# A linear-attention trunk on one core: the fourth chunk matrix made behind the solve, inverse steps over sixteen gaps, output transposes a chunk later, the last residuals in one load

## The chip, the core and the metric

One NeuronCore of a Trainium2 chip runs the whole program: TensorE (PE, with its weight loads as PEld), VectorE (DVE), ScalarE (ACT), GpSimd (POOL), and SyncE (SP), which issues most DMAs. The metric is the device time of one execution in microseconds (us). Each engine runs its instructions in the order in which they stand in its queue, and waits on semaphores.

## The reference, cut to what matters

A sequence of 2048 tokens with 1024 features is normed, modulated and projected. Half of the projection goes through a recurrent mixer (RWKV-7: 8 heads with a 64 x 64 state each), half through banded attention; both are gated, projected by `w_out`, and added to x.

```
def rwkv7_step(state, inp):
    r_t, w_t, k_t, v_t, a_t, b_t = inp
    sa = jnp.einsum('bhij,bhj->bhi', state, a_t)
    state = state * w_t[:, :, None, :] + sa[..., None] * b_t[:, :, None, :] + v_t[..., None] * k_t[:, :, None, :]
    y = jnp.einsum('bhij,bhj->bhi', state, r_t)
    return state, y
...
y = jnp.concatenate([y_r * jax.nn.silu(g_r), y_a * jax.nn.silu(g_a)], axis=-1)
x = x + gate[:, None, :] * (y @ w_out[l])
```

## The kernel before

The recurrence is computed in 32 chunks of 64 tokens (`NCH`), four to a block of 256 tokens (`NCB` = 4, `TR` = 256, `NB` = 8). Within a chunk the step over time becomes a triangular system; only the 64 x 64 state z goes from chunk to chunk. The change lies in `phase_r`, the loop over the chunks, which runs from about 1278 us to the end. What comes before it (projections, attention, and the first two blocks' matrices) is not touched.

Per block b there are these tiles and tensors: `ar` and `kb` (1 MB each, loaded from DRAM by `prefetch`), `g` (the chunk matrices, four chunks of eight heads), `l_d` and `xt_d` (small DRAM tensors through which 32 x 32 diagonal blocks change their layout). The chain that makes a block ready is:

- `qchunk(b, c)` (L191): 16 matmuls into `ps_q` and two masks on DVE (L206) make chunk c's matrix in `g`. After the fourth chunk, SP stores the diagonal blocks to `l_d` (L210, four DMAs).
- `inv(b)` (L218): SP loads a unit matrix into `xtt` (L221) and the diagonals into `lt` (L223); DVE inverts them in 31 steps of two instructions, `pd` (L229) and `xtt` (L231); SP stores the result to `xt_d` (L234) and reads it back into `g` (L237, four DMAs).
- `turn(b)` (L855): DVE transposes the inverted blocks into x. `merge1(n)` and `merge2(n)` (PE, with ACT copies between) then complete chunk n's inverse.

A chunk n runs on PE in this order: `from_state` (L891, L894, with the state z), `state_keys` for the next chunk, `solve` (L904), `merge1` of the next chunk, `state` (L912, after which DVE makes the new z, L914 and L915), `read_out` (L923), `values` for the next two chunks at odd n, `merge2`, `qchunk` of block b+2, `from_values` (L884). At the last chunk of a block (a border), `turn` and `merge1` of the next block stand late, after `read_out`.

Between these stand gaps. `gap()` does two things: it takes one step of `fill`, a generator that does the output projection (`outputs`; three matmuls of 512 columns into `ps_out`, L130 to L132, eight groups of four steps to a job), and it calls `invert()`, which takes as many steps of the inverse as its count of calls allows. There are six calls of `invert` in a chunk, so 24 in a block. The output of a pair of chunks goes through `square` (ACT) and `spread` (DVE, then POOL) after the second chunk; in the next, even chunk follow `scaled` (L942, DVE on ys), `flip` (L947, PE transposes and four ACT pieces L950 into yf), and `gated` (L955, L956, DVE, and a store to `yr_d`). The residual of each output group is loaded into one of three `xres` buffers (L1012), added on DVE (L1027), and stored by POOL's queue (L1028).

In this phase PE, DVE and ACT keep the order in which the code is written; SP and POOL are ordered by a scheduler. The two lines that pace the inverse are

```
work.update(inv=q_["inv"](b + 1) if b + 1 < NB else iter(()), calls=0, done=0)   # at the first chunk of block b
want = min(32, max(0, 5 * (work["calls"] - 4) // 2))
```

that is, inverse b+1 starts in block b at the fifth call, two and a half steps a call, and its 32nd item (the stores) falls to the 17th.

## Time and profile before

| | us |
|---|---|
| median of three runs (1746.02, 1747.77, 1752.72) | 1747.77 |
| the profiled execution | 1754.3 |
| its span, first to last instruction | 1752.5 |
| PE busy | 1564.3 (89%) |
| DVE busy | 1087.3 (62%) |
| ACT busy | 929.8 (53%) |
| mean granted TensorE clock | 0.947 |

The recurrent phase is the last quarter of the span. An engine's busy share over the whole span says little of it, since the stages before have other limits. Therefore the rows below are taken from stretches of that phase: by chunk, by block, and by the DMAs that lead from one block to the next. A granted clock of 1 is 2.4 GHz, of 0.5 it is 1.2 GHz; a mean between them says that the stretch had parts at both. In the tables of stretches, x is the number of instructions.

### The profile page before, as it was taken

The numbers are of one execution on the slowest core, as the hardware profiler recorded it, in microseconds if no ns is written. First come the engines' busy times: TensorE is split into PE (matmuls) and PEld (weight loads), VectorE is DVE, ScalarE is ACT, GpSimd is POOL, SyncE is SP. The second block draws the span as 40 slices with busy tenths as digits, with TensorE's granted clock in tenths as the row PEclk, the third lists the DMA queues.
The fourth block names the chain that finished last, engine by engine and source line by source line (L and its number), as shares of the span: only waits on it lengthen the run. The fifth ranks groups of instructions, "written<-read, shape, count | busy, mean of one in ns | idle before, by whom it ended". The sixth has DMA issues, their size and how long they took to land.

```text
span 1752.5 us, 32125 instructions
## 1 busy us (share of the span) xinstructions
PE 1564.3 (89%) x11944; PEld 1280.5 (73%) x11944; DVE 1087.3 (62%) x2435; ACT 929.8 (53%) x2087; POOL 674.2 (38%) x543
## 2 busy tenths in 40 slices
PE   3899999899999799999979999987889889988895
PEld 2677877688778678878868888866667767776775
DVE  7546457475576857557485574575965677656642
ACT  3666556566565566656656565662244344443550
POOL 4456545465454455544435543332401111111112
PEclk9899999799999999999999999998988998889998
DMA  8463332332324423132242323146576665654533
GB/s 288 122 222 101 115 111 89 128 103 86 114 85 141 158 86 127 67 109 97 79 127 78 122 76 99 55 144 197 173 221 187 176 196 159 187 163 131 151 120 99
DMA packets 188956, 231.59 MB, mean 132 GB/s; under 512 B 62976, under 2 KB 101632, under 8 KB 188800
## 3 DMA queue, kind: packets, MB, share of 16 engines
q1 hardware_dynamic: 183552, 212.76, 39.9%
q0 software_dynamic: 5248, 16.78, 2.6%
q8 instruction: 94, 1.54, 0.4%
q14 instruction: 62, 0.51, 0.1%
HBM read 171.30 MB, written 58.20 MB: 131 GB/s over the span
## 4 chain that ended last, share of the span: by engine, by line
PE 57%; DVE 21%; DMA 8%; issue 6%; ACT 4%; POOL 1%; SPq 1%; POOLq 0%; DVEq 0%; ACTq 0%
PE ps_qkvg L130 6%; PE ps_qkvg L131 6%; PE ps_qkvg L132 6%; PE ps_r L130 5%; PE ps_r L131 5%; PE ps_r L132 5%; PE ps_pt L604 2%; DVE pd L229 2%; DVE xtt L231 2%; PE ps_o L613 2%; DVE kbt L318 2%; PE ps_o L612 2%; DMA g<-xt_d 2%; PE ps_sa L567 2%; PE ps_out L130 1%
## 5 line engine op out<-in xcount | busy, mean ns | idle before, releaser
L111 POOL TENSOR_TENSOR wlo<-raw,whi 128x512 fp32r<-128x512 f32 x272 | 369.6, 1363 | 438.9 <-ACT whi L122 384.4
L122 ACT CAST whi<-raw 128x512 fp32r<-128x512 f32 x272 | 167.7, 618 | 176.8 <-issue 58.0
L130 PE MATMUL ps_r<-hh,whi 128*128 128x512 f32 x544 | 219.1, 403 | 11.1 <-ACT carry L641 9.7
L132 PE MATMUL ps_r<-hh,wlo 128*128 128x512 f32 x544 | 217.9, 401 | 2.3 <-POOL wlo L111 2.2
L131 PE MATMUL ps_r<-hl,whi 128*128 128x512 f32 x544 | 217.7, 400 | 0.0
L130 PE MATMUL ps_qkvg<-hh,whi 128*128 128x512 f32 x480 | 197.4, 413 | 11.6 <-ACT carry L641 7.3
L131 PE MATMUL ps_qkvg<-hl,whi 128*128 128x512 f32 x480 | 194.5, 406 | 7.9 <-DVE hl L386 5.5
L132 PE MATMUL ps_qkvg<-hh,wlo 128*128 128x512 f32 x480 | 193.2, 404 | 0.4 <-POOL wlo L111 0.3
L111 DVE TENSOR_TENSOR ptl<-ps_pt,pth 128x384 fp32r<-128x384 f32 (+1 forms) x232 | 105.3, 472 | 43.8 <-ACT pth L607 43.3
L597 ACT ACTIVATE sp<-sp,mn 128x640 f32<-128x640 f32 (+4 forms) x128 | 97.9, 765 | 63.8 <-DVE mn L593 62.9
L130 PEld LDWEIGHTS ps_r<-hh,whi 128*128 128x128 f32 x544 | 103.3, 190 | 31.6 <-ACT carry L641 10.6
L132 PEld LDWEIGHTS ps_r<-hh,wlo 128*128 128x128 f32 x544 | 102.9, 189 | 24.8 <-POOL wlo L111 3.1
L131 PEld LDWEIGHTS ps_r<-hl,whi 128*128 128x128 f32 x544 | 103.2, 190 | 20.1
L130 PEld LDWEIGHTS ps_qkvg<-hh,whi 128*128 128x128 f32 x480 | 92.5, 193 | 33.6 <-ACT carry L641 8.8
L131 PEld LDWEIGHTS ps_qkvg<-hl,whi 128*128 128x128 f32 x480 | 92.6, 193 | 30.3 <-DVE hl L386 7.6
L607 ACT CAST pth<-ps_pt 128x384 fp32r<-128x384 f32 (+1 forms) x232 | 90.8, 415 | 43.5 <-PE ps_pt L604 38.8
L132 PEld LDWEIGHTS ps_qkvg<-hh,wlo 128*128 128x128 f32 x480 | 92.3, 192 | 21.1 <-POOL wlo L111 0.7
L613 PE MATMUL ps_o<-ptl,vc 128*128 128x256 f32 x336 | 95.6, 309 | 9.9 <-DVE ptl L111 9.9
L604 PE MATMUL ps_pt<-cs,sp 128*128 128x128 f32 x560 | 96.9, 285 | 7.7 <-DVE ptl L111 3.3
L612 PE MATMUL ps_o<-pth,vc 128*128 128x256 f32 x336 | 94.3, 300 | 6.5 <-ACT pth L607 5.9
L591 DVE CUSTOM_DVE_ANT_0 sp<-ps_sa,mab 128x384 f32<-128x384 f32 (+1 forms) x112 | 58.7, 524 | 55.9 <-PE ps_sa L567 32.2
L1028 POOL DMA_DIRECT2D out<-xres x40 | 22.1, 554 | 176.9 <-DVE xres L1027 134.2
(257 smaller groups left out, 3702.0 us busy)
## 6 DMA issues: line engine op xcount, KB each, us to landing
raw<-in_wi SPq DMA_DIRECT2D x264, 256.0 KB, 2.9
hx<-in_xT SPq DMA_DIRECT2D x32, 256.0 KB, 5.3
wada<-in_wadaT SPq DMA_DIRECT2D x16, 512.0 KB, 8.4
ar_d<-art SPq DMA_DIRECT2D x16, 512.0 KB, 3.6
kb_d<-kbt SPq DMA_DIRECT2D x16, 512.0 KB, 3.2
kb<-kb_d SPq DMA_DIRECT2D x8, 1024.0 KB, 6.4
ar<-ar_d SPq DMA_DIRECT2D x8, 1024.0 KB, 7.0
xres<-in_xT SPq DMA_DIRECT2D x32, 256.0 KB, 3.6
```

The lines of the kernel that those rows point to most:

```text
L111: eng.tensor_tensor(out=out, in0=full, in1=hi.bitcast(F32), op=ALU.subtract)
L122: nc.scalar.copy(out=hi, in_=raw)
L130: nc.tensor.matmul(ps, lhsT=wh[:, f], rhs=hh[:, k, :], start=first, stop=False)
L131: nc.tensor.matmul(ps, lhsT=wh[:, f], rhs=hl[:, k, :], start=False, stop=False)
L132: nc.tensor.matmul(ps, lhsT=wl[:, f], rhs=hh[:, k, :], start=False, stop=last)
L229: nc.vector.tensor_tensor(out=pv_, in0=xt[:, 0:nj, s].unsqueeze(2).broadcast_to([P, nj, nt]), in1=lt[:, s, s + 1:32].unsqueeze(1).broadcas ...
L591: nc.vector.tensor_tensor_reduce(out=sp[:, 0:na], in0=sa[:, 0:na], in1=m_ap, scale=1.0, scalar=3e38, op0=ALU.add, op1=ALU.min, accum_out=m ...
L597: nc.scalar.activation(sp[:, 0:n], sp[:, 0:n], AF.Exp, scale=-1.0, bias=mn[:, 1:2], accum_out=ls[:, 2 * v + hh_:2 * v + hh_ + 1])
L604: nc.tensor.transpose(pp[:, kk - lo, :], sp[:, kk * P:(kk + 1) * P], ident)
L607: nc.scalar.copy(out=ph, in_=pp)
L612: nc.tensor.matmul(po[:, hh_, :], lhsT=wv_, rhs=pth[:, m, :], start=(m == m0), stop=False)
L613: nc.tensor.matmul(po[:, hh_, :], lhsT=wv_, rhs=ptl[:, m, :], start=False, stop=(m == 5))
```

## The change

- `qchunk` of the fourth chunk of block b+2 moves, at a border, from behind `merge2` to behind `solve`. The generator of inverse b+2 is made right there, so that its loads are issued there too. In block 0, inverse 1 is still started at the first chunk.
- `invert()` takes two steps a call, in block 0 from the third call, in the others from the first, so that 32 items lie in 16 calls.
- `flip` moves from the even chunk to the odd chunk after it, ahead of `state`; `gated` and `load_sides` follow it. `scaled` stays in the even chunk.
- In chunks 1, 5, 9, 13 and 17 one gap calls `invert()` alone and takes no step of `fill`.
- The residuals of the last 512 tokens are loaded into one tile, `ends`, by two DMAs of 1 MB each, written at chunk 26 in the code. The jobs of 256 columns then take them from there instead of loading `xres`.

```diff
@@ -966,7 +966,14 @@
         def load_sides(m):
             sides[m] = load_pair("gg", sg_d, m), load_pair("bv", bv_d, m)
 
-        wres = {}
+        wres, ends = {}, []
+
+        def load_ends():
+            ends.append(rp.tile([P, KT, 512], F32, name="ends", tag="g2", bufs=1))
+            for hf in range(2):
+                o = slice(256 * hf, 256 * hf + 256)
+                nc.sync.dma_start(out=ends[0][:, :, o], in_=xa_d[:, :, S - 512 + 256 * hf:S - 256 + 256 * hf].rearrange("m p t -> p m t"))
+
 
         def load_w(m, half):
             raw = wx.tile([P, 512], F32, name="raw", tag="raw", bufs=3)
@@ -1008,8 +1015,11 @@
                 for m in range(KT):
                     if ji == 0 and not fin and m + 2 < KT:
                         load_w(m + 2, 1)
-                    xt = rq.tile([P, 512], F32, name="xres", bufs=3)[:, 0:n]
-                    nc.sync.dma_start(out=xt, in_=src[m, :, tsl])
+                    if n < 512:
+                        xt = ends[0][:, m, t0:t0 + n]
+                    else:
+                        xt = rq.tile([P, 512], F32, name="xres", bufs=3)
+                        nc.sync.dma_start(out=xt, in_=src[m, :, tsl])
                     ps = psp.tile([P, 512], F32, name="ps_out", tag="pj")[:, 0:n]
                     if m == 6 and nxt:
                         raws = [fetch_y(nxt, k) for k in range(4)]
@@ -1034,7 +1044,7 @@
 
         jobs = [(b, 1, 0, 512) for b in (1, 2, 3)] + [(b, 0, 0, 512) for b in (0, 1, 2)] + [(3, 0, 0, 256)]
         fill = outputs(jobs, False)
-        work = dict(inv=iter(()), calls=0, done=0)
+        work = dict(inv=q_["inv"](1), calls=0, done=0, lag=2)
 
         def gap(steps=True):
             next(fill, None)
@@ -1043,7 +1053,7 @@
 
         def invert():
             work["calls"] += 1
-            want = min(32, max(0, 5 * (work["calls"] - 4) // 2))
+            want = min(32, 2 * max(0, work["calls"] - work["lag"]))
             while work["done"] < want:
                 next(work["inv"], None)
                 work["done"] += 1
@@ -1066,12 +1076,15 @@
             pend = None
             for n in range(NCH):
                 b, c = divmod(n, NCB)
+                if n == NCH - 6:
+                    load_ends()
                 even, more, border = n % 2 == 0, n + 1 < NCH, n % NCB == NCB - 1
                 if c == 0:
                     if b + 2 < NB:
                         q_["prefetch"](b + 2)
-                    work.update(inv=q_["inv"](b + 1) if b + 1 < NB else iter(()), calls=0, done=0)
-                    next(work["inv"], None)
+                    work.update(calls=0, done=0, lag=2 if b == 0 else 0)
+                    if b == 0:
+                        next(work["inv"])
                 pb = from_state(n, z)
                 if more:
                     state_keys(n + 1)
@@ -1079,27 +1092,36 @@
                 solve(n, pb)
                 if more and not border:
                     merge1(n + 1)
+                if border and b + 2 < NB:
+                    q_["qchunk"](b + 2, c, psm)
+                    work["inv"] = q_["inv"](b + 2)
+                    next(work["inv"])
+                    work["done"] = 32
                 if even and more:
                     vfs[n // 2 + 1] = load_vf(n // 2 + 1) if n + 2 < NCH else None
                 gap()
                 if even and pend is not None:
                     scaled(*pend[1:])
                 gap()
+                flipped = None
+                if not even and pend is not None:
+                    flipped = pend[0], flip(pend[1])
                 zn = state(n, z)
                 if even:
                     ys = rp.tile([P, 8, 64], F32, name="ys", bufs=2)
                 read_out(n, ys)
                 z = zn
-                if even and pend is not None:
-                    yf = flip(pend[1])
                 if not even:
                     ysq = square(ys)
                     if more:
                         values(n + 1)
+                if n % 4 != 1 or n > 20:
+                    gap()
+                else:
+                    invert()
                 gap()
-                gap()
-                if even and pend is not None:
-                    gated(pend[0], yf)
+                if flipped:
+                    gated(*flipped)
                     load_sides(n // 2)
                 if more and border:
                     turn(b + 1)
@@ -1107,7 +1129,7 @@
                 gap(False)
                 if more:
                     merge2(n + 1)
-                if b + 2 < NB:
+                if b + 2 < NB and not border:
                     q_["qchunk"](b + 2, c, psm)
                 invert()
                 if not even:
```

What stands on SP around the border of block 4 (chunk 19). Before, from the store of the inverse of block 5 on (`g_15043` is that block's matrix, `g_15798` the one of block 6):

```order
L234 DMA xt_d<-xtt 1024x1x32 x2
L819 DMA bv<-bv_d 128x4x128
L959 DMA yr_d<-yf 128x4x128
L819 DMA gg<-sg_d 128x4x128
L1012 DMA xres<-xa_d 128x512
L237 DMA g_15043<-xt_d 32x16x32 x4
L173 DMA ar_16367<-ar_d 128x4x512
L221 DMA xtt<-in_eyes 128x512
L264 DMA vf<-v_d 128x4x128
L1012 DMA xres<-xa_d 128x512 x2
L210 DMA l_d<-g_15798 32x16x32 x4
L223 DMA lt<-l_d 64x1024 x2
```

The same place on SP in the changed kernel (`g_15028` and `g_15780` are the same two matrices):

```order
L234 DMA xt_d<-xtt 1024x1x32 x2
L1022 DMA xres<-xa_d 128x512
L237 DMA g_15028<-xt_d 32x16x32 x4
L221 DMA xtt<-in_eyes 128x512
L173 DMA ar_16340<-ar_d 128x4x512
L1022 DMA xres<-xa_d 128x512
L210 DMA l_d<-g_15780 32x16x32 x4
L223 DMA lt<-l_d 64x1024 x2
L819 DMA bv<-bv_d 128x4x128
L959 DMA yr_d<-yf 128x4x128
L819 DMA gg<-sg_d 128x4x128
```

The loads of the sides and the store of yf now stand behind lt, and l_d stands three transfers behind the readback of g instead of five.

DVE at the beginning of block 4 (chunk 16) before, from the turn of the border on (`x` is the turned diagonal; `pd` and `xtt` are steps of the inverse of block 5):

```order
L855 STREAM_TRANSPOSE x_12606<-g_14300 32x512 x2
L1027 SCALAR_TENSOR_TENSOR xres<-ps_out,modv,xres 128x512
L206 TENSOR_TENSOR g_15043<-ps_q,cs 128x4x128 x2
L935 TENSOR_REDUCE s_15641<-ysq 128x8
L936 TENSOR_SCALAR s_15641<-s_15641 128x8
L942 TENSOR_TENSOR ys<-ys,rsg 128x512
L914 TENSOR_TENSOR z<-ps_z,z 128x256
L915 TENSOR_TENSOR z<-z,wcall 128x256
L1027 SCALAR_TENSOR_TENSOR xres<-ps_out,modv,xres 128x512
L229 TENSOR_TENSOR pd<-xtt,lt 128x31
L231 TENSOR_TENSOR xtt<-xtt,pd 128x31
```

The same place on DVE in the changed kernel, from the first step of that inverse to the chunk's z:

```order
L229 TENSOR_TENSOR pd<-xtt,lt 128x58
L231 TENSOR_TENSOR xtt<-xtt,pd 128x2x29
L229 TENSOR_TENSOR pd<-xtt,lt 128x56
L231 TENSOR_TENSOR xtt<-xtt,pd 128x2x28
L942 TENSOR_TENSOR ys<-ys,rsg 128x512
L111 TENSOR_TENSOR yl_15710<-yraw,yh_15709 128x512
L111 TENSOR_TENSOR wrl_15716<-raw,wrh_15715 128x512
L229 TENSOR_TENSOR pd<-xtt,lt 128x81
L231 TENSOR_TENSOR xtt<-xtt,pd 128x3x27
L229 TENSOR_TENSOR pd<-xtt,lt 128x78
L231 TENSOR_TENSOR xtt<-xtt,pd 128x3x26
L914 TENSOR_TENSOR z<-ps_z,z 128x256
```

Steps 3 to 6 are shown; the first two stand just ahead of these. Before, no step stood ahead of this z; now six do, and the first of them waits for lt.

## Rows read from the trace of the kernel before

**Rows 1.** Stretches of chunks 9 to 11: length, busy time by engine, granted clock, DMA.

```profile
core 0: us, PE busy (x) PEld busy (x) DVE busy (x) ACT busy (x) POOL busy (x), PEclk, DMA share, GB/s
1404.78:1416.20 11.42, 11.42 (x180) 9.44 (x178) 10.46 (x36) 6.43 (x17) 0.54 (x1) 1.00 0.53 161
1416.20:1431.80 15.60, 12.18 (x176) 9.95 (x174) 14.71 (x44) 7.08 (x18) 3.12 (x3) 0.89 0.64 190
1431.80:1449.91 18.11, 15.01 (x180) 12.03 (x178) 6.76 (x12) 6.95 (x18) 1.08 (x2) 0.78 0.87 246
```

**Rows 2.** Waits of PE, 1272 to 1690 us: total us, times, longest us.

```profile
PE ps_mg L862 <- DVE x L855: 19.6, 8, 3.8
PE ps_yf L947 <- DVE pd L229: 10.4, 4, 2.9
PE ps_yf L947 <- DVE ys L942: 9.7, 3, 3.4
```

**Rows 3.** SP's timeline: start us, us of issuing, what, count.

```profile
1275.47 1.13 SPq L223 DMA_DIRECT2D lt<-l_d  x2
...
1487.15 1.27 SPq L234 DMA_DIRECT2D xt_d<-xtt  x2
...
1491.28 2.18 SPq L237 DMA_DIRECT2D g<-xt_d  x4
...
1496.13 0.40 SPq L173 DMA_DIRECT2D ar<-ar_d  x1
...
1508.13 2.64 SPq L210 DMA_DIRECT2D l_d<-g  x4
1512.39 1.13 SPq L223 DMA_DIRECT2D lt<-l_d  x2
```

**Rows 4.** DMA issues of 1487 to 1497 us, lt's of 1507 to 1517: us to landing.

```profile
ar<-ar_d SPq DMA_DIRECT2D x1, 1024.0 KB, 7.2
...
g<-xt_d SPq DMA_DIRECT2D x4, 64.0 KB, 5.0
...
vf<-v_d SPq DMA_DIRECT2D x1, 256.0 KB, 7.5
...
lt<-l_d SPq DMA_DIRECT2D x2, 256.0 KB, 3.8
```

**Rows 5.** Stretches between the DMAs of two blocks, and chunk 29; columns as in rows 1.

```profile
1517.00:1543.17 26.17, 24.44 (x378) 20.00 (x378) 23.84 (x79) 11.98 (x35) 3.51 (x5) 1.00 0.61 187
1600.86:1669.65 68.79, 58.95 (x822) 47.43 (x820) 39.88 (x107) 30.20 (x81) 9.76 (x11) 0.88 0.58 156
1319.38:1600.86 281.48, 248.72 (x3422) 202.17 (x3420) 185.66 (x506) 125.00 (x335) 33.77 (x40) 0.90 0.62 174
1679.57:1689.54 9.97, 9.97 (x164) 8.18 (x162) 3.33 (x6) 5.81 (x17) 0.86 (x2) 1.00 0.71 208
```

**Rows 6.** Groups on DVE, 1459.4 to 1487 us: count, busy us, mean ns, idle before.

```profile
L111 DVE TENSOR_TENSOR wrl<-raw,wrh 128x512 fp32r<-128x512 f32 x3 | 2.1, 686 | 0.2 <-ACT wrh L978 0.2
L915 DVE TENSOR_TENSOR z<-z,wcall 128x256 f32<-128x256 f32 x2 | 0.9, 426 | 0.1
...
L942 DVE TENSOR_TENSOR ys<-ys,rsg 128x512 f32<-128x512 f32 x1 | 0.7, 681 | 0.0
```

**Rows 7.** PE's timeline around chunk 11: start us, us, what, count.

```profile
1430.19 1.16 PE L203 MATMUL ps_q<-ar,kb 64*128 64x128 f32 x16
...
1435.04 0.39 PE L131 MATMUL ps_out<-yl,whi 128*128 128x512 f32 x1
1435.27 0.40 PE L132 MATMUL ps_out<-yh,wlo 128*128 128x512 f32 x1
```

**Rows 8.** Waits from 1700 us to the end; columns as in rows 2.

```profile
DVE xres L1027 <- DMA xres<-xa_d: 15.3, 9, 3.0
...
PE ps_out L130 <- ACT fin L963: 4.2, 1, 4.2
...
PE ps_yf L947 <- DVE ys L942: 2.1, 1, 2.1
```

**Rows 9.** Waits of SP's queue, 1480 to 1520 us; columns as in rows 2.

```profile
SPq L1012 <- DMA xa_d<-xres: 14.2, 3, 6.5
```

## What I predict

> **What bounds the kernel now.** I cut the recurrent part (chunks 0 to 31, 1278.5 to about 1709 us) at the first from_state matmul of each chunk, then read the waits of PE, then SP's timeline. Block 2 (chunks 8 to 11) stands for the others. Chunk 9 takes 11.42 us with PE busy throughout [rows 1]. Chunk 10 takes 15.60 and chunk 11 18.11, with PE busy 12.18 and 15.01 and the granted clock at 0.89 and 0.78: part of each runs at the 1.2 GHz level, right after PE has stood still. PE's waits have two names [rows 2]: merge1 at a border waits for the turned diagonal x (19.6 us), and the flip for the scaled ys, directly or behind a step of the inverse on DVE (9.7 and 10.4 us).
>
> Why x is late is a loop from one block's inverse to the next [rows 3]. The store of the result (xt_d) is issued at 1487.15, its readback into g at 1491.28, the 1 MB load of ar at 1496.13, the next block's diagonals (l_d) only at 1508.13, since qchunk stands at the end of the border chunk, and lt, from which the next inverse starts, at 1512.39. The second lt goes out about 0.5 later and lands after 3.8 [rows 4], at 1516.7. From there to the next store DVE is busy 23.84 of 26.17 us [rows 5]; the rest is 79 gaps of 0.03. So a block is a **lap** over SP and the DMA queue, 29.6 us here, plus a **stretch** on DVE, 26.4: 56.0. The five periods from the store at 1319.38 to that at 1600.86 take 281.48 us [rows 5], 56.3 each. PE alone needs four chunks of about 11.3, 45 us: it isn't the bound.
>
> **Part 1, the fourth matrix behind the solve.** At a border qchunk moves from behind merge2 to behind solve, and the diagonals' stores and the next inverse's loads with it. Its 16 matmuls (1.16 us [rows 7]) are not new; ahead of merge1 they give the turn that much more cover. What it can shorten is the lap. SP's order is now: store, at most an xres and two yraw, readback, eyes, ar, at most an xres, l_d, lt. The three transfers bv, yr_d and gg no longer stand between store and readback, and l_d no longer waits for the chunk's end; but it now stands behind ar. Sum: readback 4.1 us after the store (it waits for the landing, as now); ar issued at about 8; landed at about 14 (7.2 behind its issue in [rows 4], less about 1 for the three transfers gone); l_d's four behind it at 15.5; lt issued by 16.7 and landed 3.8 to 4.3 later, at 21. Ends: 17 if l_d doesn't queue behind ar, 30 if SP is held as long as now. That it queues is what [rows 4] show: vf, 256 KB and issued right behind ar, landed after 7.5 us, not before the megabyte ahead of it. I take 21.
>
> The Trainium skill (DMA: Bandwidth & Descriptors, section Queues, rings and completion order) says that a DMA engine consumes descriptors in ring order, but that completion is not FIFO per issuing engine. By the second statement alone l_d could land ahead of ar and the lap would be at its lower end; the vf row of this trace speaks for the first.
>
> **Part 2, the inverse over sixteen gaps.** Its 62 instructions stay. They start at a block's first gap instead of the fifth, and end one gap sooner. But DVE runs in order, so between first and last step there is more of its other work. For the same inverse (of block 5, made in block 4) the order adds to the stretch of [rows 5] one z update (two instructions of 0.42), one scaled (0.68) and three splits (0.69 each) [rows 6]: 3.6 us, so 26.4 + 3.6 = 30. In the other blocks it adds 0.8 to 3.3; I keep 30, and 27 to 32 as ends. There is also a new wait: a step that needs lt now stands ahead of chunk 4b's z, and queued behind it on DVE are scaled, z and the evictions of ps_out. With lt landing some 8 us into the chunk and six steps, a scaled and two or three splits ahead of z, z is ready after 13 us, where PE wants it after 10 for the next from_state. I expect PE to stand 2 to 4 us there, about 2 more for the border chunk's z, and the clock to fall behind some of these. All that lies inside the 30.
>
> **Period.** 21 + 30 = 51 us, 5.3 less than 56.3. PE's own path, 45 us, some 3 lost at the lower clock and 2 of merging at the border, makes 50: it doesn't decide, but it is next. Five periods: 5 x 5.3 = **-26.5 us**.
>
> **Part 3, transposes a chunk later.** The flip follows scaled by a whole chunk, so its 20.1 us of waits [rows 2] go. Nothing of that is counted again: inside the five periods it only lets PE keep up with DVE. ACT gets four yf pieces more in an odd chunk, beside 6.43 busy of 11.42 [rows 1], and loses them in an even one: nothing, as long as ACT has that room. Gated moves along, and load_sides behind it on SP. One fill is skipped in chunks 1, 5, 9, 13 and 17: three matmuls 0.23 apart [rows 7], 0.7 us, hidden in the loop by DVE; they come back behind the loop, 3.5 us, paid in part 5.
>
> **Part 4, before and behind the five periods.** Block 1's inverse starts from lt issued at 1275.47 [rows 3], landed by 1280; it now takes two steps a call from the third call, about 1282.5; 29.6 of DVE work and 2 of idle put its store at 1314, not 1319.4: **-5** (0 to -7). From the sixth store to chunk 28 it is 68.79 us now [rows 5]. After: readback 4.1, landing 5.0 [rows 4], two transposes 1.4, so merge1 at 10.5, and 3.5 to the next chunk; chunks 24 to 26, without masks, 30 (an odd one without flip takes 9.97 [rows 5]); chunk 27 13.5. That is 57.5: **-11** (-5 to -14).
>
> **Part 5, the last residuals.** At the end the 256-column residuals take turns through three buffers: DVE waits 15.3 us for their loads, PE 4.2 for fin behind these evictions and 2.1 for ys [rows 8]. From ends, loaded ahead (2 MB around chunks 23 to 26; it may put some us on lt of the last inverse, whose stretch lacks the masks and has that room), the evictions follow PE at once. Counted: 2.1, of fin's 4.2 some 1.5 (gated and cast stay), about 4 in the last job where evictions wait for loads, less 3.5 for the fills that return: **-4** (-1 to -8).
>
> Sum: -26.5 - 5 - 11 - 4 = -46.5. The profiled execution took 1754.3 us (span 1752.5), 6.5 over the median of 1747.77. Against the profiled execution the sum gives 1754.3 - 46.5 = 1707.8; a timed run is compared with the median, so I forecast 1747.8 - 46.5, some **1701**.
>
> **Rivals.** (a) **A shorter lap**: l_d doesn't queue behind ar, the lap is 17, PE's 48 becomes the period, the waits for z go: 3 less in each of five periods and 4 in block 6, 1682. Against it: the vf row. (b) **The lap stays**: SP is in order, and an xres between ar and l_d waits for an earlier eviction's store, 6.5 us at the longest now [rows 9]. Lap 28, stretch 30, period 58: five times 1.7 lost, 15 kept of parts 4 and 5, 1741. (c) **Slower**: the wait for lt ahead of z feeds itself. From a lap of 31 lt lands 17 us into the chunk and holds z, the evictions, and through their stores SP's own xres and l_d. Period 61: 5 x 4.7 = 23.5 lost against 11 kept, 1760. SP's 6.5 and a lap as now would just reach it; that l_d's wait for the chunk's end is gone speaks against. (d) **The inverse isn't sooner**: the last step stands right behind z of chunk 4b+2, and with PE late there by its waits and the lower clock the store follows PE. Period 54, 1716.
>
> **How the numbers follow.** Forecast 0.50, (d) 0.20, (a) 0.13, (b) 0.10, (c) 0.07. One us in the period is 5 in the time; periods of 48 to 55.5 give 1686 to 1724, and head and tail some 5 either way: 1678 to 1727, which takes in (a) and (d). Within 0.5%, about what a measurement of this kernel can tell from no change, is 1739 to 1756.5. Faster by more: the forecast, (a), (d) and a third of (b), 0.86; same 0.08; slower 0.06.
>
> **What would show it.** Stores of xt_d about 51 us apart; lt landed 21 behind each, right behind ar; DVE busy from there to the next store; no flip waiting for ys; new waits of from_state for z in chunks 4b+1 and 4b+3; no eviction at the end waiting for a load. I am wrong if stores stay 55 apart or more, or if l_d lands ahead of ar.

## The result and the profile after

The changed kernel takes 1729.82 us, the median of four runs (1723.63 to 1733.57), beside 1750.24 of the kernel before on the same chip. The ratio is 0.9867, with a 95% interval of 0.9822 to 0.9911: faster by 20 us, where the prediction had 46.5 and a range that ended at 1727. The profiled execution has a span of 1729.9, 22.6 less than before.

That the stores of xt_d come closer together is right, but they do so by a third of what was forecast. The first row below is the five periods from the store at 1317.47 us to that at 1590.69, 273.22 us where they were 281.48 [rows 5]; the second is the stretch on DVE of block 2, the third the time from the sixth store to chunk 28, where 68.79 stood. Stretches of the changed kernel, columns as in rows 1:

```profile
1317.47:1590.69 273.22, 240.49 (x3330) 196.29 (x3325) 181.96 (x501) 123.47 (x330) 32.32 (x38) 0.90 0.63 175
1392.66:1422.99 30.33, 26.95 (x374) 22.33 (x376) 27.03 (x85) 13.90 (x37) 3.95 (x5) 0.89 0.51 162
1590.69:1652.51 61.82, 56.37 (x858) 45.45 (x857) 40.84 (x108) 32.00 (x88) 9.40 (x12) 0.99 0.77 197
```

The lap did become shorter. SP's timeline of the changed kernel at the border of block 2, to be laid beside rows 3:

```profile
1422.99 2.27 SPq L234 DMA_DIRECT2D xt_d<-xtt  x2
...
1428.10 2.00 SPq L237 DMA_DIRECT2D g<-xt_d  x4
...
1432.45 0.38 SPq L173 DMA_DIRECT2D ar<-ar_d  x1
...
1434.22 2.40 SPq L210 DMA_DIRECT2D l_d<-g  x4
1440.70 1.13 SPq L223 DMA_DIRECT2D lt<-l_d  x2
```

From store to the second lt's issue it is 18.2 us, where it was 25.7 at the border of [rows 3]. And l_d does land behind ar, as the vf row of [rows 4] had it; that it waits there for ar is tested in experiment 4. The landings of 1422 to 1445 us, to be read with these issues:

```profile
ar<-ar_d SPq DMA_DIRECT2D x1, 1024.0 KB, 5.6
...
lt<-l_d SPq DMA_DIRECT2D x2, 256.0 KB, 3.8
...
l_d<-g SPq DMA_DIRECT2D x4, 64.0 KB, 4.8
```

The megabyte landed at 1438.1; the diagonals, issued 1.8 to 3.5 behind it, from 1439.2 on, in the order of their issue. The Trainium skill (DMA: Bandwidth & Descriptors, section Queues, rings and completion order) also has it that completion is not FIFO per issuing engine; on SP's queue no landing here overtook the megabyte ahead of it.

What took the place of the flip's waits is seen in the chunks. Chunks 8 to 11 of the changed kernel, columns as in rows 1:

```profile
1383.93:1401.11 17.18, 13.31 (x171) 10.76 (x170) 7.77 (x27) 3.96 (x12) 0.90 (x2) 0.80 0.62 167
1401.11:1413.33 12.22, 12.22 (x180) 10.23 (x179) 10.41 (x31) 7.20 (x20) 0.78 (x2) 0.94 0.27 88
1413.33:1423.78 10.45, 10.45 (x172) 8.48 (x170) 9.64 (x30) 6.19 (x15) 2.27 (x2) 1.00 0.83 257
1423.78:1443.30 19.52, 13.96 (x184) 11.23 (x182) 9.04 (x16) 7.66 (x20) 2.74 (x3) 0.83 0.87 219
```

Chunk 10 runs without a wait now (15.60 before). But chunk 8, the block's first, has 3.9 us in which PE stands, and chunk 11, the border, 5.6; parts of both run at the 1.2 GHz level, the mean granted clock being 0.80 and 0.83. The waits of PE, 1272 to 1690 us, columns as in rows 2, give them names (merge2 stands behind the chunk's z here, so the first row is the wait for z):

```profile
PE ps_mh L873 <- DVE z L914: 14.8, 11, 4.9
PE ps_mg L862 <- DVE x L855: 9.5, 3, 5.1
PE ps_mg L862 <- issue: 7.3, 7, 4.4
```

Before, beside rows 2:

```profile
PE ps_mg L862 <- issue: 2.5, 5, 0.6
PE ps_mh L873 <- DVE z L914: 0.8, 2, 0.4
```

No flip waits any more, and z costs 14.8, where it cost 0.8. The row "issue" is merge1 too, in waits for which the profile names no releaser; its longest, 4.4 us in chunk 15, is one for x (experiment 3 shows DVE there). So merge1's waits of these two names fell less than the row for x alone says, from 22.1 to 16.8. In block 2's first chunk DVE waited 11.3 us for lt with z behind it. This is the wait that the prediction described, and in its size: lt landed 8.7 us into the chunk (some 8 forecast), and PE stood 3.9 (2 to 4 forecast).

The tail went as forecast: from chunk 31 to the end it is 47.8 us instead of 53.5, and DVE at the end follows PE, not the loads of [rows 8]:

```profile
DVE ends L1037 <- PE ps_out L132: 16.8, 16, 2.1
```

### The profile page after: what moved, and what is told of

It reads as the page before. It is cut to its first block, busy times and chain, and to the rows that moved or that the text cites. A ratio compares the mean times of both kernels' runs of the same rounds, so it can differ in the third digit from the quotient of the medians.

```text
span 1729.9 us, 32057 instructions
## 1 busy us (share of the span) xinstructions
PE 1550.2 (90%) x11944; PEld 1269.1 (73%) x11944; DVE 1086.2 (63%) x2435; ACT 929.4 (54%) x2087; POOL 673.2 (39%) x543
## 4 chain that ended last, share of the span: by engine, by line
PE 57%; DVE 21%; DMA 10%; issue 5%; ACT 4%; POOL 1%; SPq 1%; POOLq 0%; DVEq 0%; ACTq 0%
PE ps_qkvg L130 6%; PE ps_qkvg L131 6%; PE ps_qkvg L132 6%; PE ps_r L130 5%; PE ps_r L131 5%; PE ps_r L132 5%; PE ps_pt L604 2%; DVE pd L229 2%; DVE kbt L318 2%; DVE xtt L231 2%; PE ps_o L613 2%; PE ps_out L130 2%; PE ps_o L612 2%; DMA lt<-l_d 2%; DMA l_d<-g 1%
## 5 line engine op out<-in xcount | busy, mean ns | idle before, releaser
L122 ACT CAST whi<-raw 128x512 fp32r<-128x512 f32 x272 | 167.5, 618 | 175.8 <-issue 53.7
L130 PEld LDWEIGHTS ps_r<-hh,whi 128*128 128x128 f32 x544 | 103.6, 191 | 33.5 <-ACT carry L641 11.2
L229 DVE TENSOR_TENSOR pd<-xtt,lt 128x126 f32<-128x126 f32 (+22 forms) x248 | 67.9, 274 | 51.5 <-DMA lt<-l_d 46.1
```

The costliest lines, as they stand in the source:

```text
L122: nc.scalar.copy(out=hi, in_=raw)
L130: nc.tensor.matmul(ps, lhsT=wh[:, f], rhs=hh[:, k, :], start=first, stop=False)
L229: nc.vector.tensor_tensor(out=pv_, in0=xt[:, 0:nj, s].unsqueeze(2).broadcast_to([P, nj, nt]), in1=lt[:, s, s + 1:32].unsqueeze(1).broadcas ...
```

## The experiments

Two measures are used. *Five periods* is the time from the second to the seventh store of xt_d in the trace (the first two belong to the head; the seventh is the one that the prediction calls the sixth), and its mean is parted into lap and stretch as in the prediction. It holds a shift where the pacing changes between block 0 and the others; therefore *chunks 4 to 24*, from the first from_state of chunk 4 to that of chunk 24, stands beside it. The last column is the ratio times 1750.2, the kernel before's median beside the changed kernel, so that runs of different chips can be compared.

| | ratio, 95% interval | lap, stretch | five periods | chunks 4 to 24 | us at 1750.2 |
|---|---|---|---|---|---|
| before | 1 | 28.1, 28.2 | 281.5 | 282.7 | 1750.2 |
| changed | 0.9867 [0.9822, 0.9911] | 22.4, 32.2 | 273.2 | 277.3 | 1726.9 |
| 1 flip back | 0.9903 [0.9882, 0.9924] | 23.4, 30.9 | 271.2 | 273.9 | 1733.2 |
| 2 old pacing | 0.9830 [0.9811, 0.9850] | 22.3, 31.4 | 268.5 | 267.1 | 1720.4 |
| 3 splits later | 0.9832 [0.9809, 0.9855] | 22.9, 30.2 | 265.1 | 267.7 | 1720.8 |
| 4 ar behind lt | 0.9823 [0.9800, 0.9846] | 19.5, 32.9 | 261.9 | 267.2 | 1719.2 |
| 5 half the inverse | 0.9744 [0.9722, 0.9767] | 23.0, 28.5 | 257.4 | 262.0 | 1705.4 |
| 6 matrix late again | 1.0056 [1.0034, 1.0078] | 28.4, 31.5 | 299.6 | 301.9 | 1760.0 |
| 7 = 3 and 4 | 0.9715 [0.9691, 0.9738] | 19.9, 29.8 | 248.3 | 251.4 | 1700.3 |
| 8 = 7, steps behind z | 0.9756 [0.9730, 0.9781] | 16.4, 35.1 | 257.6 | 258.2 | 1707.5 |
| 9 part 1 alone | 0.9881 [0.9858, 0.9904] | 23.2, 29.3 | 262.3 | 262.1 | 1729.4 |
| 10 without part 5 | 0.9935 [0.9909, 0.9961] | 22.3, 32.8 | 275.2 | 278.3 | 1738.8 |
| 11 = 7, behind z, 17th call | 0.9712 [0.9684, 0.9740] | 19.0, 31.1 | 250.5 | 248.6 | 1699.8 |
| 12 half, in eight calls | 0.9787 [0.9759, 0.9816] | 31.8, 16.1 | 239.6 | 258.8 | 1712.9 |
| 13 parts 1 and 5 | 0.9872 [0.9845, 0.9900] | 23.2, 29.8 | 264.9 | 267.3 | 1727.8 |
| 14 = 11, flip back | 0.9701 [0.9673, 0.9729] | 19.3, 29.4 | 243.2 | 244.5 | 1697.9 |

The five blocks of experiments 9 and 13 are the same code but for the loads of `ends`, and differ by 5.2 us; those of the changed kernel and experiment 10 differ by 1.0. Each comes from one execution. A difference of chunks 4 to 24 under 5 us is therefore not read as one; two pairs of kernels are all that this bound rests on. The changed kernel's ratio has the widest interval of all, so its parts are weighed by these blocks rather than by its median.

### What each part is worth (experiments 6, 9, 10, 13, 1 and 2)

**Experiment 6** undoes part 1.

```diff
...
-                if border and b + 2 < NB:
-                    q_["qchunk"](b + 2, c, psm)
-                    work["inv"] = q_["inv"](b + 2)
...
-                if b + 2 < NB and not border:
+                if b + 2 < NB:
                     q_["qchunk"](b + 2, c, psm)
```

> The changed kernel with part 1 undone: the fourth matrix and the loads of the next inverse stand at the end of the border chunk again; pacing over sixteen gaps, flip and residuals as changed. Theory A: the lap goes back to 28 to 30 while the stretch stays at 32, so the period is 60 to 62, above that of the kernel before, and the time 1757 to 1765 (the third of the rivals of the prediction, made on purpose). Rival B (PE's path): lt comes some 7 us later into the chunk, z waits for it longer, but the stretch shrinks by the waits that then lie ahead of it: period 56 to 57, time 1737 to 1743.

Measured 1765.07 us beside 1755.77, slower than before. Five periods:

```profile
1309.51:1609.12 299.61, 251.70 (x3336) 205.56 (x3331) 182.14 (x502) 123.56 (x330) 32.29 (x38) 0.87 0.57 159
```

Lap 28.4, as in the kernel before, and stretch 31.5: 59.9, at the lower end of theory A's. So the other parts without part 1 make the kernel slower, with nearly the period of the prediction's rival (c), 61. The lap of 31 on which that rival rested did not occur; the lap stayed, and the stretch grew.

**Experiment 9** makes part 1 alone, in the kernel before.

```diff
...
+                if border and b + 2 < NB:
+                    q_["qchunk"](b + 2, c, psm)
+                    work["inv"] = q_["inv"](b + 2)
+                    next(work["inv"])
+                    work["done"] = 32
...
-                if b + 2 < NB:
+                if b + 2 < NB and not border:
                     q_["qchunk"](b + 2, c, psm)
```

> The kernel before with part 1 alone: the fourth matrix and the loads of the next inverse behind the solve; pacing, flip, gaps and residuals as before. Theory A (part 1 shortens the lap from 28.1 to 22.4 us, the stretch stays at 28.2): period 50.6 instead of 56.3, five periods -28 and the stretch behind the sixth store -6: 1713 to 1721, faster than the whole change. Rival B (the period needs parts 2 and 3 too, since the flip's waits grow when DVE carries the steps sooner): period 53 to 55, time 1732 to 1740.

Measured 1731.51 us: between the two, and as fast as the whole change. Its chunks 4 to 24, and after it the same chunks of the changed kernel:

```profile
1334.84:1596.97 262.13, 234.02 (x3446) 189.81 (x3444) 185.00 (x504) 124.13 (x335) 33.67 (x41) 0.97 0.68 186
```

```profile
1329.94:1607.22 277.28, 245.63 (x3432) 200.58 (x3432) 183.32 (x503) 124.52 (x334) 32.47 (x39) 0.91 0.63 173
```

Part 1 takes 20.6 us from these blocks (282.7 before), and the rest of the change gives 15.2 of them back: PE stands 3.5 us longer (the length less PE's busy time), and its matmuls take 11.6 us more, at a lower clock (0.91 beside 0.97). With experiment 13 in its place, whose blocks are the same code, part 1 takes 15.4 and 10.0 come back. The change makes this up at its ends: the last chunk's tail is 47.8 here and 54.7 there.

**Experiment 10** undoes part 5 (xres instead of `ends`, no `load_ends`).

```diff
-                    if n < 512:
-                        xt = ends[0][:, m, t0:t0 + n]
-                    else:
-                        xt = rq.tile([P, 512], F32, name="xres", bufs=3)
-                        nc.sync.dma_start(out=xt, in_=src[m, :, tsl])
+                    xt = rq.tile([P, 512], F32, name="xres", bufs=3)[:, 0:n]
+                    nc.sync.dma_start(out=xt, in_=src[m, :, tsl])
```

> The changed kernel with part 5 undone: the last residuals take turns through three buffers again. Theory A (the 5.7 us between the start of the last chunk and the end are the residuals'): chunk 31 to the end 53 to 54 instead of 47.8, time 1733 to 1737. Rival B (the two megabytes of the load ahead cost as much on the last inverse as they save at the end): stretch of the sixth period 25 instead of 27.2, and 1728 to 1731.

Measured 1740.34 us. The last chunk to the end takes 57.4 us, 9.6 more than in the changed kernel, and DVE's waits there have the name of [rows 8] again:

```profile
DVE xres L1034 <- DMA xres<-xa_d: 17.0, 9, 4.0
```

Theory A, and larger: part 5 is worth 9.6 in the tail (against the kernel before the skipped gaps come off, which both of these kernels have there), and the stretch of the last inverse, 26.4 beside 27.2, says that the loads ahead cost the loop at most a microsecond in this order of SP.

**Experiment 2** undoes the pacing of part 2 only.

```diff
-            want = min(32, 2 * max(0, work["calls"] - work["lag"]))
+            want = min(32, max(0, 5 * (work["calls"] - 4) // 2))
```

> The changed kernel with the old pacing (first step at the fifth call of a block, two and a half steps a call, store at the seventeenth), while the fourth matrix stays behind the solve, so that lt is loaded as early as now. Theory A (lap plus stretch on DVE): the steps start some 4 us after lt has landed and the store comes a call later, so a period grows by 2 to 3 us: five periods 284 to 288, time 1740 to 1745. Rival B (what holds the chunks is z standing behind the wait for lt, 14.8 us of PE's waits in the changed kernel): those waits go, the periods shrink to 51 to 52, time 1715 to 1722.

Measured 1720.73 us, rival B's number. Chunks 4 to 24, then chunk 8 and chunk 10 by themselves:

```profile
1328.70:1595.79 267.09, 238.59 (x3435) 194.65 (x3432) 184.47 (x504) 124.47 (x335) 32.68 (x39) 0.94 0.65 180
...
1380.18:1390.63 10.45, 10.45 (x173) 8.48 (x170) 3.19 (x9) 4.12 (x13) 0.75 (x2) 1.00 0.58 152
1402.24:1416.97 14.73, 11.84 (x172) 9.64 (x170) 13.84 (x43) 6.19 (x15) 2.27 (x2) 0.92 0.68 211
```

The first chunk falls from 17.18 to 10.45 us at full clock, and the third rises from 10.45 to 14.73, since DVE carries the steps there: the five first chunks of blocks 1 to 5 lose 22.6 us together, the third ones gain 14.1. So the pacing over sixteen gaps moved PE's wait from the third chunk to the first, and the one in the first is dearer: the five blocks are 10.2 us longer with it. Of these 10.2, PE's standing is 3.2 (277.28 less 245.63 there, 267.09 less 238.59 here); the other 7.0 are as many matmuls at a lower clock (0.91 beside 0.94). Rival B holds by half: the wait at the first chunk goes, but the periods are 53.7, not 51 to 52, and z costs 14.2 us in all beside 14.8, as it is waited for in the third chunk again.

**Experiment 1** undoes part 3 (flip and gated in the even chunk; the skipped gaps stay).

```diff
-                flipped = None
-                if not even and pend is not None:
-                    flipped = pend[0], flip(pend[1])
...
+                if even and pend is not None:
+                    yf = flip(pend[1])
```

> The changed kernel with part 3 undone: flip and gated stand in the even chunk again, everything else as changed. Theory A (a period is a lap over the queue of 22.4 us plus a stretch on DVE of 32.2 us, 54.6): the flip only uses PE time inside the loop, so the five periods stay within 1 us each of 54.6 and the time is 1724 to 1738. At the border chunks ACT loses the four yf pieces (1.50 us) that now stand ahead of the casts for which DVE waits 3.6 us in front of the turn, so PE's wait for the turned x may shrink by 1 to 2 us there. Rival B (PE's own path sets the period): the 20.1 us of flip waits of the kernel before come back and the time is 1740 to 1750.

Measured 1733.12 us, theory A. 36.3 us of flip waits come back on PE, and nearly all waits for z go in exchange:

```profile
PE ps_yf L947 <- DVE pd L229: 26.5, 7, 7.0
PE ps_mg L862 <- DVE x L855: 9.9, 4, 3.5
PE ps_yf L947 <- DVE ys L942: 9.8, 4, 5.1
PE ps_mh L873 <- DVE z L914: 1.4, 2, 1.0
PE ps_mg L862 <- issue: 1.0, 2, 0.6
```

PE waits for the same DVE under another name. The guess that x would come sooner at the borders holds for chunks 11 and 15, though the row for x, 9.9 us instead of 9.5, hides it: merge1 stood 5.1 and 4.4 us there in the changed kernel, the second without a releaser's name, and 3.3 and 2.7 here; with the row "issue" its waits fall from 16.8 to 10.9. In chunk 3 it stands longer, 3.5 for 1.7. Less of it is ACT's four pieces than the guess had: in chunk 15 the subtraction ahead of the turn waits 3.17 us for its cast instead of 3.62, and the other 1.4 are gated's two instructions on DVE, which no longer stand ahead of the turn.

**Experiment 13** has parts 1 and 5 without parts 2 and 3 (the diffs of experiments 1 and 2, and all gaps take a fill).

```diff
-                if n % 4 != 1 or n > 20:
-                    gap()
-                else:
-                    invert()
+                gap()
```

> The kernel before with parts 1 and 5 alone: fourth matrix behind the solve and the last residuals in one load; pacing, flip and gaps as before. From part 1 alone (1731.5 us, last chunk to end 54.7) and the tail of the changed kernel (47.8, of which 3.5 are its skipped gaps) the time should be 1721 to 1725, if parts add. Theory D (part 3, the flip a chunk later with its skipped gaps, is worth nothing or less once part 1 is there): as fast as the second experiment, which has part 3 besides (1720.7), or faster: 1716 to 1722. Rival (part 3 is worth the flip's 20.4 us of PE waits): 6 us or more slower than the second experiment, 1727 to 1735.

Measured 1727.95 us, where the sum of parts had 1721 to 1725 and experiment 2 took 1720.73; the intervals of the two ratios overlap by a hair (0.9845 to 0.9900, and 0.9811 to 0.9850). The rival's number, but not its place: chunks 4 to 24, where the flip's waits stand, take 267.3 us without part 3 and 267.1 with it. What part 3 may be worth, up to 7 us, lies in chunks 0 to 4 (53.0 against 51.2) and 24 to 28 (51.9 against 46.2), less 3.6 for the gaps in the tail; that it is part 3's wasn't shown.

### What the period consists of (experiments 3, 4, 7, 5 and 12)

**Experiment 3** puts the subtraction of a split two gaps behind its cast. In the changed kernel they stand back to back in two queues, and where a step of the inverse is behind the subtraction, it waits with it. DVE in chunk 12 of the changed kernel, start us and us (in brackets the idle time ahead):

```profile
1445.41 0.19 DVE L229 TENSOR_TENSOR pd<-xtt,lt 128x31 f32<-128x31 f32 x1 [5.45 <-DMA lt<-l_d]
...
1446.09 0.19 DVE L231 TENSOR_TENSOR xtt<-xtt,pd 128x30 f32<-128x30 f32 x1
1449.73 0.69 DVE L111 TENSOR_TENSOR wlo<-raw,whi 128x512 fp32r<-128x512 f32 x1 [3.46 <-ACT whi L985]
1450.34 0.21 DVE L229 TENSOR_TENSOR pd<-xtt,lt 128x58 f32<-128x58 f32 x1
```

```diff
             nc.scalar.copy(out=hi, in_=raw)
-            sub(nc.vector, lo, raw, hi)
+            subs.append([2 * live[0], lambda: sub(nc.vector, lo, raw, hi)])
+            if not live[0]:
+                subs.pop()[1]()
...
+        def step():
+            next(fill, None)
+            live[0] = 1
+            for s in list(subs):
+                s[0] -= 1
+                if s[0] < 0:
+                    s[1]()
+                    subs.remove(s)
```

> The changed kernel with one edit: the subtractions of the splits (wlo, wrl, yl) stand two gaps behind their casts on ACT, not right behind them. Same instructions. Theory A (the stretch of 32.2 instead of the forecast 30 is DVE's waiting for those casts, 0.9 to 4.2 us in a stretch): the stretch falls to 30, the period to 52.4, and the turn of two borders comes 2 to 3 us sooner: time 1712 to 1719. Rival B (DVE has time to spare there, PE's path sets the store): the wait comes back as a wait for z, g or ps_out, the period stays at 54 to 55, time 1726 to 1734.

Measured 1720.05 us, a microsecond beside theory A's range. The stretch is 30.2, as A had it, and no stretch has a wait for a cast any more (11.6 us in the five of the changed kernel, 2.3 each: 0.9, 0.3, 4.2, 2.8 and 3.4). Two borders gain more than that: in chunks 11 and 15 the turn of x had stood behind such a subtraction. DVE in chunk 15 of the changed kernel:

```profile
1491.66 0.69 DVE L111 TENSOR_TENSOR wrl<-raw,wrh 128x512 fp32r<-128x512 f32 x1 [3.62 <-ACT wrh L985]
1492.27 0.69 DVE L955 TENSOR_TENSOR yf<-yf,bv 128x512 f32<-128x512 f32 x1
1492.98 0.69 DVE L956 SCALAR_TENSOR_TENSOR yf<-yf,gg 128x512 f32<-128x512 f32 x1
1493.71 1.43 DVE L855 STREAM_TRANSPOSE x<-g 32x512 f32<-32x512 f32 x2
```

Chunk 15 of the changed kernel as a whole, then chunks 11 and 15 with splits later:

```profile
1480.38:1499.26 18.88, 13.86 (x185) 11.17 (x182) 8.37 (x15) 8.80 (x22) 0.54 (x1) 0.88 0.73 180
```

```profile
1418.13:1434.80 16.67, 13.86 (x185) 11.14 (x182) 9.65 (x17) 7.67 (x20) 2.74 (x3) 0.87 0.95 258
1469.08:1482.08 13.00, 12.18 (x185) 9.86 (x183) 9.10 (x16) 8.58 (x22) 1.92 (x3) 1.00 0.82 211
```

Chunk 11 takes 2.9 and chunk 15 5.9 us less. Part of it comes back, as rival B says: PE waits 6.7 us for subtractions that now stand behind DVE's wait for lt, most of it in chunk 16.

**Experiment 4** loads ar behind lt.

```diff
...
-        with (tc.issue_after(diag_dma[0].ins) if b > 1 else nullcontext()):
+        with (tc.issue_after(lt_dma[0].ins) if b > 1 else nullcontext()):
...
```

> The changed kernel with one edit: the 1 MB load of ar is issued behind lt instead of ahead of l_d. Theory A (l_d queues behind the megabyte, and the lap counts in full): l_d lands some 3 to 3.5 us behind its issue, lt is issued at about 11 behind the store and the lap falls from 22.4 to 16 or 17; the period falls to 49 to 50, time 1705 to 1711. Rival B (the lap falls, but the stretch grows by the same as DVE then waits for PE and ACT): period 53 to 54, time 1722 to 1730. Rival C (the transfers share the engines whatever their order): lap 21 to 23, time 1726 to 1734.

Measured 1720.40 us, between A and B. SP's timeline at the border of block 1:

```profile
1360.92 1.44 SPq L234 DMA_DIRECT2D xt_d<-xtt  x2
1366.68 1.94 SPq L237 DMA_DIRECT2D g<-xt_d  x4
...
1369.67 3.40 SPq L210 DMA_DIRECT2D l_d<-g  x4
1375.53 1.13 SPq L223 DMA_DIRECT2D lt<-l_d  x2
...
1377.39 0.45 SPq L173 DMA_DIRECT2D ar<-ar_d  x1
```

The lap falls by 2.9 to 19.5, not to 17: the readback alone is issued 5.8 behind the store, where the prediction had 4.1, and lt 5.9 behind the first l_d. The stretch grows by 0.7. So ar ahead of l_d costs 3 us of the lap, and rival (a) of the prediction, the lap of 17, isn't reached even without it.

**Experiment 7** has both edits.

> The changed kernel with the two edits of the third and fourth experiment together: subtractions of the splits two gaps behind their casts, ar behind lt. Theory A (lap and stretch add, and neither edit touches the other's term): lap 19.5, stretch 30.2, period 49.7, five periods 248, time 1703 to 1709. Rival B (PE's own path is reached before that): period 51 to 52, time 1711 to 1716.

Measured 1706.29 us beside 1755.77: A, and by the ratio a little more. Lap 19.9 and stretch 29.8 make 49.7, so the two terms do add. Chunks 4 to 24:

```profile
1323.64:1575.00 251.36, 233.50 (x3435) 189.96 (x3432) 182.48 (x504) 124.69 (x335) 33.47 (x40) 0.97 0.68 192
```

**Experiments 5 and 12** ask whether DVE's arithmetic sets the stretch. In both, every second step of the inverse is left out from block 2 on; experiment 12 also takes four items a call.

```diff
         for s in range(31):
+            if s % 2 and b > 1:
+                yield
+                continue
...
-            want = min(32, 2 * max(0, work["calls"] - work["lag"]))
+            want = min(32, work["rate"] * max(0, work["calls"] - work["lag"]))
...
```

> The changed kernel, in which every second step of the inverse (two instructions) is left out from block 2 on; so this part of the computation is missing, and the rest stands as it was. 15 of 31 steps of some 0.51 us go, 7.6 us and a microsecond of gaps. Theory A (lap plus stretch decides): the stretch falls from 32.2 by all of it, and the period from 54.6 to 46 to 48, where PE's own path takes over: 1690 to 1700. Rival B (PE's waits at the border for x and behind the wait for lt decide, which the arithmetic does not touch): period 51 to 53, time 1712 to 1722.

> The changed kernel, in which every second step of the inverse is left out from block 2 on (that part of the computation is missing) and the rest is taken at four items a call, so that the store falls to the eighth call, not the sixteenth. DVE's work in a call is that of the changed kernel. In the fifth experiment, with as many steps left out but sixteen calls, the stretch stayed at 28.5 us. Theory C (the stretch can't be shorter than PE needs for the sixteen gaps among which the steps stand, some 28 us; DVE's 30 is only a little above): now the stretch falls to 14 to 17, x is ready ahead of each border, and PE's own path is left: period 46 to 48, time 1683 to 1693. Theory A as first put (DVE's work alone makes the stretch): as the fifth experiment, 1705 to 1713.

Experiment 5: 1711.90 us beside 1755.77, on rival B's side; by the ratio 1705.4, between the two. The stretch fell by 3.7 us, not by 8: with DVE at half its steps it is as long as PE needs for the gaps among which they stand. Experiment 12: 1715.62 us; the stretch falls to 16.1, as theory C has it, and yet chunks 4 to 24 take 258.8 us, not to be told from experiment 5's 262.0 and far from theory C's 46 to 48 a block. Both theories missed the time. What is left on PE in those blocks, 1270 to 1690 us, is a wait of merge1 for which the profile shows no releaser, and z; then chunks 11 and 15:

```profile
PE ps_mg L865 <- issue: 12.6, 9, 5.1
PE ps_mh L876 <- DVE z L917: 10.5, 8, 3.1
```

```profile
1418.48:1438.00 19.52, 13.96 (x185) 11.24 (x182) 9.06 (x18) 7.66 (x20) 2.74 (x3) 0.82 0.82 236
1473.38:1492.26 18.88, 13.98 (x185) 11.27 (x182) 8.37 (x15) 8.79 (x22) 0.54 (x1) 0.83 0.72 207
```

Chunks 11 and 15 are as long as in the changed kernel, although their x was stored a chunk sooner. So those two borders do not wait for the inverse at all, but for DVE's queue ahead of the turn, as experiment 3 showed (here too a subtraction stands ahead of each turn and waits 3.6 us for its cast); and z still stands behind lt. With splits later this kernel wasn't run.

### Kernels that go further (experiments 8, 11 and 14)

**Experiment 8** starts the steps of experiment 7 behind z (`lag=3` in all blocks), at two a call.

> The kernel of the seventh experiment with one more edit: the first step of every inverse stands at the fourth call of a block, behind z of the first chunk, still two a call, so that the store falls to the nineteenth call. Theory A (lap plus stretch on DVE): steps start later than lt lands, the store comes up to 6 us later in its block, so the period grows by 1 to 3 us against the seventh: 5 to 15 us more. Rival B (the steps ahead of z make PE stand 2 to 4 us at each block's start, and half of that is lost again at the lower clock): without them the period falls to 47 to 49, time 1693 to 1703.

Measured 1713.90 us, A: 7.6 more than the seventh. z costs 1.1 us now, but the store, at the border's first call, makes the readback late for the turn:

```profile
PE ps_mg L862 <- DMA g<-xt_d: 16.3, 7, 4.3
```

**Experiment 11** starts there as well, and takes 2.4 a call, so that the store comes two calls sooner.

```diff
-            want = min(32, 2 * max(0, work["calls"] - work["lag"]))
+            want = min(32, 12 * max(0, work["calls"] - work["lag"]) // 5)
```

> The kernel of the seventh experiment (splits later, ar behind lt) with the steps beginning at the fourth call, behind z, at 2.4 a call, so that the store falls to the seventeenth call. Theory A (lap plus stretch; the store one call later than the sixteenth, and more steps to a call): period 49.5 to 51, time 1703 to 1710, as the seventh. Rival B (z's waits of 8.9 us and the lower clock behind them count in full, and the store isn't what PE waits for): 1691 to 1699.

Measured 1702.13 us, ratio 0.9712: as the seventh. **Experiment 14** undoes part 3 in it.

> The kernel of the eleventh experiment (splits later, ar behind lt, steps behind z, store at the seventeenth call) with part 3 undone: flip and gated in the even chunk, no gap skipped. Theory D (the flip's waits only use time in which PE would wait for the loop anyhow): 1696 to 1706, as the eleventh. Rival (here lap and stretch are short enough for PE's own path to count, so the flip's waits of some 20 us come back in full): 1712 to 1722.

Measured 1698.26 us, ratio 0.9701, the fastest of all and, by its interval, not to be told from experiments 7 and 11. The flip's waits come back with 14.5 us, and chunks 4 to 24 still lose nothing, so theory D holds:

```profile
1324.78:1569.31 244.53, 229.15 (x3447) 185.35 (x3444) 183.98 (x504) 123.85 (x335) 34.40 (x41) 0.99 0.72 199
```

It has a fault of its own: in block 6 both loads of `ends` were issued right ahead of lt, which landed 11.0 us behind its issue instead of 3.8 [rows 4], and chunks 24 to 28 took 52.2 us, where experiment 11 took 45.3. How much of this is the load isn't shown: in the same chunks 2.4 us are a flip that waits for ys, which experiment 11 doesn't have.

```profile
ends<-xa_d SPq DMA_DIRECT2D x2, 1024.0 KB, 8.8
lt<-l_d SPq DMA_DIRECT2D x2, 256.0 KB, 11.0
```

## Why the prediction was wrong, step by step

Faster was right, and so was the picture: a lap over SP and the queue, a stretch on DVE, and a change whose worth is in the lap. The size was wrong, mostly in one term, the five periods: the stretch was given no time for DVE's waits, the start of z behind lt was taken as hidden, and lap and stretch were read from the block with the longest lap and the shortest stretch of the five.

- **Five periods: forecast -26.5, measured -8.3.** This is 18 of the 24 us missing. The period is 54.6 us (lap 22.4, stretch 32.2), forecast 51 (21 and 30).
- **The base of the two terms.** One lap and the stretch behind it, in block 4, 29.6 and 26.4, stood for all. Over the five periods before they were 28.1 and 28.2: the sum is the same, the parts are not. The lap shown was the longest of the five and the stretch the shortest, so the lap promised 1.5 us too much, and the stretch started 1.8 too low.
- **Lap, 22.4 for 21.** The order of its parts was right, l_d behind ar included (experiment 4: 3 us). The term that was too small is the first: in the five laps the readback was issued 3.8 to 7.6 behind the store, 5.4 in the mean, not 4.1, since the store itself landed as late; what held the store wasn't tested. Before, the readback was issued after 4.1 to 5.2, so taking bv, yr_d and gg from between the two gained nothing there. The gain is l_d, issued 17.5 to 21.0 behind the store before and 7.6 to 11.2 now.
- **Stretch, 32.2 for 30.** The step that failed by its mechanism: the sum counted what DVE does between first and last step, 3.6 us more, and no wait. In the mean of the five, DVE's busy time in a stretch grew by 1.8 us only (25.8 to 27.6), and its waits for other engines by 2.3 (0.4 to 2.7). With the steps from the first gap on, subtractions of the splits stand among them and wait 2.3 us a stretch for ACT's casts, where it was 0.3 before. Without these waits the stretch is 30.2 (experiment 3).
- **"All that lies inside the 30."** Wrong as well. The wait for z, which stands behind lt, was foreseen with 2 to 4 us (3.9 in chunk 8), and taken as hidden in the loop; it costs. With the old pacing, the first step behind z and the store a call later, five blocks are 10.2 us shorter (experiment 2). The loop isn't lap plus DVE's work alone: a stretch can't be shorter than PE's gaps (experiment 5), and a block not than PE's waits at its first chunk and its border (experiment 12).
- **Part 3: "the 20.1 us of its waits go".** They went, and z took their place; that nothing was counted for it was right (experiments 1 and 14). "ACT: nothing" did not hold at two borders: in chunks 11 and 15 the flip's pieces and gated stand ahead of the turn, and undoing the move took 1.8 us of merge1's wait in each, in chunk 15 some 0.45 of it by ACT (experiment 1).
- **Part 4, head.** Forecast -5, measured -1.9 at the second store; chunk 0 began 1.6 later in this execution, at 1280.1 us, so that it is 3.5 from there. With splits later the first period in the trace is 54.1 instead of 56.3 us, so the casts are 2.2 of it.
- **Part 4, sixth store to chunk 28.** Forecast 57.5, measured 61.8. Chunks 24 to 26 took the 30 us, but began 16.5 behind the store instead of 14.0, and chunk 27 took 15.3 for 13.5. The sum led to chunk 24 by the store's way back; it was PE that came later: chunk 23 began 3.6 behind the store and took 13.0, PE busy for 12.2 of them at full clock.
- **Part 5.** Forecast -4, measured -5.7, by the mechanism named (experiment 10).

The rivals: (b) and (c) did not occur, and experiment 6 shows that without part 1 the period would have been about (c)'s. Rival (d) had the period, 54, but not the reason: in five blocks the store followed z of the third chunk within 0.3 to 1.7 us, yet in four of them DVE, not PE, made z late (chunk 10: z ready 3.7 us behind state's first matmul, where a chunk without a queue on DVE takes 1.6). What stays open is what the early flip is worth at the loop's ends, 0 to 7 us (experiments 2 and 13), and why the five blocks of part 1 alone came out at 262.1 and at 267.3 us in two kernels that differ by two loads. The stores came 54.6 us apart: the prediction's own sign of being wrong, 55 or more, was set too far out to show this miss.

## What to carry to other kernels

Part a loop into its terms over all its rounds, not from one, even where the sum of that one is right. Where steps of a long chain are spread among other instructions of an in-order engine, ask of each neighbour whether its input is ready at that place: an operation that only follows a cast on another engine holds the chain as long as the cast is late, and moving it two places back took 9.6 us out of five blocks here. And undo the parts one by one: here part 1 carried the gain in the loop, the new pacing spent 10 us of it, and the early flip gave nothing there that these runs can tell.

## What the runs showed of the hardware

PE's own busy time is no constant of the work. Chunks 4 to 24 hold 3444 matmul records with 249.7 us of PE busy before, at a mean granted clock of 0.90, and 3447 with 229.2 in experiment 14, at 0.99: where PE stands, matmuls behind the stand run at the 1.2 GHz level for a time. They do not do so in proportion: with the flip back (experiment 1) PE stands 38.2 us in these chunks, beside 31.7 in the changed kernel, and yet its 3432 matmuls take 235.6 us instead of 245.6, at 0.94 instead of 0.91. Before, these chunks read:

```profile
1337.73:1620.46 282.73, 249.69 (x3444) 203.03 (x3444) 185.17 (x505) 124.48 (x334) 33.76 (x40) 0.90 0.60 169
```

So a floor for PE that counts in the lower clock of a kernel that waits is too high: the prediction's 50 us a block, 3 of them for the lower clock, was undercut by experiment 14's 48.9. And a load of 2 MB, put ahead to save waits at the end, tripled the landing time of the small load behind it, 11.0 us for 3.8.
